# Pacing the background sums of an f32 network: the steps of three weight sums leave the leads and the widening stages

## The chip, the cores and the metric

One core of one Trainium2 chip runs the whole program. The metric is the device time of one launch in microseconds (us); the figure before is the median of three runs. The chip's engines are named as in the profile: PE (TensorE matmul), PEld (its weight load), DVE (VectorE), ACT (ScalarE), POOL (GpSimd), SP (SyncE, here only a DMA queue).

## The reference

Three transformer-like layers on 512 positions of width 1024, all in f32:

```
h = x + concat(conv_group(rmsnorm(x) @ w_in), pool_group(...)) @ w_out        # the "mixer"
h = h + swiglu(rmsnorm(h), w_gate, w_up, w_down)        # d_ff = 2816
x = rmsnorm(h)
x = layer_norm(ALPHA * x + fox_attention(x))        # first attention, 16 heads
x = layer_norm(ALPHA * x + conv_ffn(x))        # 2816 * 2 wide, 3-tap causal convolution, silu(g) * v
k1, k2, v = shared_kv(x)
x = layer_norm(ALPHA * x + diff_attention(x, k1, k2, v))        # second attention, 8 heads
x = layer_norm(ALPHA * x + conv_ffn(x))
```

So there are three feed-forward blocks. Each has a widening product (1024 to 2 x 2816) and a narrowing one (2816 to 1024).

## The kernel before

**Arithmetic.** Every f32 operand is split into a high part in fp32r (ACT, L183) and a low remainder (DVE or POOL, L185), and each product is three matmuls (L436 to L438). A weight *piece* of 128 x 1024 is converted by `_convert` into `wh` and `wl`; `piece` keeps two pieces converted ahead, and `wp` holds four. Weights arrive through `raw` buffers on the SP queue.

**Two-by-two products.** The widening and narrowing products use a seven-product scheme (seven block products in place of eight), which needs sums of blocks. On the widening side, `wide` first runs a *lead* of four chunks with plain products (`f_phase(LEAD, evac)`, tile `fa`), during which POOL builds nine sums of the activations (`sums`, tile `hT`). Then 18 chunks follow (`fast_chunk`, tiles `c` and `p`). Each of the 18 needs weight sums: one add by a DMA on POOL's queue (L274, `raw<-raw`, 512 KB) and two POOL additions (L176, `raw<-raw`).

On the narrowing side (`down`, tile `dn`) the weight sums are 32 *background steps* per feed-forward block, made by `mixed(n)`: the weights are in four quarters, and sixteen steps `copy` a quarter's part in DRAM (704 KB, ACT's queue, L145), eight steps `add` another quarter to a copied part (704 KB, an accumulating DMA on POOL's queue, L152, `mixed<-in_narrow`), and eight add one sum to another (`mixed<-mixed`). Before each `add` POOL copies one column of the newest converted piece (`paced<-wh`, L150), so that the step waits for that conversion.

**What paces the steps.** `mix` runs at the end of every `_convert`: inside `with self.mixing(pace, n)` each conversion adds `pace` to a debt, and each whole unit of debt pops one step, `n` at most (32 if not given). Outside such a block `pace` is 0 and no step is issued. All 32 steps of a block must be out before its narrowing weights are loaded (`halves`, an assert).

Before, the steps of the first sum (`mixed(0)`) are issued in the mixer (input product, output product) and then in the first block's widening stage. Those of `mixed(1)` start in the first narrowing stage (16), go on in the first attention's output product (8) and end in the next lead (8). Those of `mixed(2)` start in the second narrowing stage (16) and go on in the second attention's value product and output product (8 each).

**The mixer.** For each of four channel groups, `conv` forms a 31-tap causal convolution: a first share of the taps goes to PE as products with diagonal matrices (ACT writes them, L644 and L645, `diagonals`), a second to ACT and POOL (ACT scales, L666, `pr<-u`; POOL adds, L176, `part<-part,pr`: 10, 10, 10 and 8 of them and one more per group for PE's share), the rest to DVE (L671, `cacc`). `conv_norm` then needs all four groups (`cv`, L682), and PE's output product follows.

Instructions are put on each engine's queue by a list scheduler from the program order and priorities; an engine takes its queue in that order.

Of the kernel before, what the change touches and what calls it, by code (L numbers as in the profile page):

```python
# [25 lines left out]
KD = D // P  # L26
# [12 lines left out]
LEAD = 4  # L39
# [60 lines left out]
class Net:  # L100
# [73 lines left out]
    def pool(self, *args, **kw):  # L174

        self.pooled = self.nc.gpsimd.tensor_tensor(*args, **kw)  # L176
        return self.pooled
# [400 lines left out]
    def block1_mix(self, g):  # L578
        nc, tc, a = self.nc, self.tc, self.a
        with ExitStack() as es:  # L580
# [153 lines left out]

            with self.mixing(1):
                self.f_phase(6, evac, lead=1)
# [35 lines left out]

            with self.mixing(1):
                self.t_phase(KD, lambda k, half: ysel(k), out, order=MIX_ORDER, tail=8, pin=True)

    def wide(self, hT, evac):

        with ExitStack() as fs:
            pool, self.fz = (fs.enter_context(self.tc.tile_pool(name=n, bufs=1)) for n in ("sums", "fz"))
            with self.mixing(1):  # L780
                self.f_phase(LEAD, evac)

# [170 lines left out]
    def block1_ffn(self):  # L953
        nc, tc, a = self.nc, self.tc, self.a
        with ExitStack() as es:
            pool = lambda name, bufs=1: es.enter_context(tc.tile_pool(name=name, bufs=bufs))
            hT = pool("hT").tile([P, NF, S], F32, name="hT")
# [8 lines left out]

            with self.mixing(.5):
                self.wide(hT, evac)
            self.mixed(1)
# [5 lines left out]

            with self.mixing(.5, 16):
                self.down(es, hT, lambda x, ps, op: nc.vector.tensor_tensor(x, x, ps, op=op), done)
# [12 lines left out]
    def conv_ffn(self, layer, last):  # L990
        nc, tc, a = self.nc, self.tc, self.a
        with ExitStack() as es:
            pool = lambda name, bufs=1: es.enter_context(tc.tile_pool(name=name, bufs=bufs))
            hT = pool("hT").tile([P, NF, S], F32, name="hT")
# [16 lines left out]

            with self.mixing(.5):
                self.wide(hT, evac)
            if not last:
                self.mixed(2)
            g, b = self.row(R_FG + layer), self.row(R_FB + layer)
            done = partial(self.ln_last, g=g, b=b) if last else partial(self.ln_xt, g=g, b=b, n=1)
            with self.mixing(.5, 16):
                self.down(es, hT, lambda x, ps, op: nc.vector.scalar_tensor_tensor(x, x, ALPHA, ps, op0=ALU.mult, op1=op), done, last)
# [81 lines left out]
    def fox(self):  # L1101
        nc, tc, a = self.nc, self.tc, self.a
        with ExitStack() as es:
# [31 lines left out]

            self.t_phase(KD, lhs_v, v_out, tail=2, head=4)

# [87 lines left out]
            steps = self.fast_projections([q_done, k_done], g)  # L1225
            go = lambda n: [next(steps, None) for _ in range(n)]
# [25 lines left out]
    def diff(self):  # L1252
        nc, tc, a = self.nc, self.tc, self.a
        with ExitStack() as es:
# [122 lines left out]
            steps = chain(self.projections([q_done, k_done] * 8), begin())  # L1377
            go = lambda n: [next(steps, None) for _ in range(n)]
            go(40)
# [163 lines left out]
```

## Time and profile before

| | |
|---|---|
| median of 3 runs | 1836.85 us (1834.62 to 1841.59) |
| the profiled execution | 1831.9 us, of which the span is 1830.1 us |
| granted clock, mean | 0.974 |
| PE, DVE, ACT, POOL busy | 94%, 79%, 55%, 46% of the span |
| mixer | 16 to 185 us |
| first widening: lead, gap, 18 chunks | 184.8, 230.7, 240.8 to 449.3 us |
| first narrowing | 449 to 556 us |
| first attention, with value and output products | 556 to 828 us |
| second widening | 828.5 to 1081 us |
| second narrowing | 1081 to 1200 us |
| second attention, with value and output products | 1200 to 1464 us |
| third widening | 1464.5 to 1702.8 us |
| third narrowing | 1703 to 1817 us |

A stage's boundaries are read from the first and last matmul on its tile. The rows from the trace in the section below are of this one profiled execution. In a table by stretch the columns after the stretch are its length and, for each engine, busy us and number of instructions; the last three are the granted PE clock (1.00 is full), the mean busy share of the 16 DMA engines, and the GB/s that they moved.

### The profile page before, as it was taken

What the parts mean: (1) busy time and instruction counts of PE and PEld (TensorE: products, weight loads), DVE (VectorE), ACT (ScalarE), POOL (GpSimd) and SP (SyncE); (2) the same over time, 40 slices, a digit from 0 to 9 for tenths busy, and PEclk for the clock granted to TensorE, in tenths of its full rate; (3) what the DMA queues carried; (4) which work ended last, traced back from release to release, by engine and by line L of the source; (5) the groups of instructions that cost most, each with busy time, mean ns of one, the idle gap of its engine ahead of it and who ended that gap; (6) DMA issues with size and microseconds to landing.
All of it is one profiled execution on the core that took longest, in us unless ns stands there. A gap on an engine that the chain in (4) does not pass through costs nothing. (4 is left out here: it accounts for less than half of the span.)

```text
span 1830.1 us, 28063 instructions
## 1 busy us (share of the span) xinstructions
PE 1715.1 (94%) x10432; PEld 1500.8 (82%) x10432; DVE 1453.0 (79%) x2177; ACT 1011.7 (55%) x1733; POOL 837.1 (46%) x578
## 2 busy tenths in 40 slices
PE   7988968999999999998799999999999989999987
PEld 6767968999887788788799987777777789999865
DVE  5985544678987688878698899973888579989999
ACT  6753333455654577745365665464667455666652
POOL 2661843433506365317455555324231265655671
PEclk9998978999999999999899999999999999999999
DMA  6433788667984554666767679677333555676643
GB/s 225 149 115 138 197 183 200 191 176 224 327 269 158 136 160 131 178 158 163 175 166 194 172 241 313 236 194 203 104 96 95 137 151 137 187 191 190 204 150 112
DMA packets 106073, 326.06 MB, mean 178 GB/s; under 512 B 9888, under 2 KB 10016, under 8 KB 93904
## 3 DMA queue, kind: packets, MB, share of 16 engines
q1 hardware_dynamic: 73088, 215.53, 34.8%
q0 software_dynamic: 25648, 73.54, 21.5%
q10 hardware_dynamic: 7200, 35.20, 5.4%
q8 instruction: 82, 1.34, 0.3%
q14 instruction: 55, 0.45, 0.1%
HBM read 274.91 MB, written 73.43 MB: 190 GB/s over the span
## 5 line engine op out<-in xcount | busy, mean ns | idle before, releaser
L185 DVE TENSOR_TENSOR wl<-raw,wh 128x1024 fp32r<-128x1024 f32 (+1 forms) x415 | 561.4, 1369 | 176.7 <-ACT wh L183 173.3
L183 ACT ACTIVATE wh<-raw 128x1024 fp32r<-128x1024 f32 x457 | 449.5, 997 | 425.6 <-PE c L437 69.2
L436 PE MATMUL c<-xh,wh 128*128 128x256 f32 x992 | 288.5, 291 | 31.9 <-ACT wh L183 16.9
L176 POOL TENSOR_TENSOR raw<-raw 128x512 f32<-128x512 f32 x124 | 184.5, 1488 | 265.5 <-DMA raw<-raw 233.2
L438 PE MATMUL c<-xh,wl 128*128 128x256 f32 x992 | 285.7, 288 | 2.0 <-DVE wl L185 2.0
L437 PE MATMUL c<-xl,wh 128*128 128x256 f32 x992 | 285.0, 287 | 0.0
L436 PEld LDWEIGHTS c<-xh,wh 128*128 128x128 f32 x992 | 194.7, 196 | 35.9 <-ACT wh L183 17.7
L438 PEld LDWEIGHTS c<-xh,wl 128*128 128x128 f32 x992 | 194.8, 196 | 2.7 <-DVE wl L185 2.7
L437 PEld LDWEIGHTS c<-xl,wh 128*128 128x128 f32 x992 | 194.9, 196 | 0.1
L437 PE MATMUL dn<-wl,hh 128*128 128x512 f32 x462 | 183.1, 396 | 8.4 <-DVE wl L185 8.2
L438 PE MATMUL dn<-wh,hl 128*128 128x512 f32 x462 | 181.8, 394 | 4.3 <-DVE hl L185 4.3
L436 PE MATMUL dn<-wh,hh 128*128 128x512 f32 x462 | 181.1, 393 | 0.0
L176 POOL TENSOR_TENSOR hT<-hT 128x256 f32<-128x256 f32 (+2 forms) x66 | 147.2, 2273 | 60.1 <-DVE hT L909 54.1
L176 POOL TENSOR_TENSOR wl<-raw,wh 128x1024 fp32r<-128x1024 f32 (+1 forms) x42 | 94.3, 2250 | 117.0 <-ACT wh L183 117.0
L436 PE MATMUL fa<-xh,wh 128*128 128x256 f32 (+1 forms) x400 | 135.7, 339 | 11.5 <-DVE hT L1003 9.8
L437 PE MATMUL fa<-xl,wh 128*128 128x256 f32 (+1 forms) x400 | 134.4, 336 | 1.1 <-DVE xl L185 1.1
L438 PE MATMUL fa<-xh,wl 128*128 128x256 f32 (+1 forms) x400 | 134.2, 335 | 0.5 <-DVE rs_t L326 0.5
L176 POOL TENSOR_TENSOR rs_r<-rs_t,mhalf 128x1 f32<-128x1 f32 (+1 forms) x40 | 29.8, 747 | 226.9 <-DVE rs_t L326 223.5
L437 PEld LDWEIGHTS dn<-wl,hh 128*128 128x128 f32 x462 | 87.4, 189 | 32.8 <-DVE wl L185 15.2
L274 POOL DMA_DIRECT2D raw<-raw x62 | 76.5, 1234 | 75.5 <-DMA raw<-in_w_qk_dram 29.0
L438 PEld LDWEIGHTS dn<-wh,hl 128*128 128x128 f32 x462 | 87.6, 190 | 22.9 <-DVE hl L185 5.2
L176 POOL TENSOR_TENSOR hT<-hT,tv 128x512 f32<-128x512 f32 x44 | 82.7, 1879 | 44.7 <-DVE tv L1003 30.3
(302 smaller groups left out, 4567.2 us busy)
## 6 DMA issues: line engine op xcount, KB each, us to landing
raw<-in_w_conv_dram SPq DMA_DIRECT2D x36, 1024.0 KB, 5.0
mixed<-in_narrow_dram ACTq DMA_DIRECT2D x48, 704.0 KB, 5.7
raw<-raw POOLq DMA_DIRECT2D x62, 512.0 KB, 5.1
raw<-mixed SPq DMA_DIRECT2D x51, 512.0 KB, 5.6
raw<-in_narrow_dram SPq DMA_DIRECT2D x48, 512.0 KB, 4.9
raw<-in_w_ffn_dram SPq DMA_DIRECT2D x18, 1024.0 KB, 4.9
mixed<-in_narrow_dram POOLq DMA_DIRECT2D x24, 704.0 KB, 10.8
mixed<-mixed POOLq DMA_DIRECT2D x24, 704.0 KB, 10.3
```

Of the source, the lines that this page charges most:

```text
L176: self.pooled = self.nc.gpsimd.tensor_tensor(*args, **kw)
L183: self.copied = self.nc.scalar.activation(hi, src, AF.Copy)
L185: return self.copied, sub(lo, src, hi.bitcast(F32), op=ALU.subtract)
L274: self.nc.gpsimd.dma_start(out=raw[:, 0:4:2, :], in_=raw[:, 1:4:2, :], accum_op=ALU.add)
L436: mm(ps, lh, rh, start=first, stop=False)
L437: mm(ps, lh, rl, start=False, stop=False)
L438: mm(ps, ll, rh, start=False, stop=last)
```

## The change

The steps are the same; where they are issued changes. In the mixer the pace rises from 1 to 1.8 (input product) and 1.9 (output product), so that all 32 steps of `mixed(0)` are out before its end. The three leads and the widening stages lose their `mixing`. The narrowing stages go from pace .5 and at most 16 steps to .6 and 19. The first attention's value product gets 5 steps, and the projections in the second attention's loop run at .25.

```diff
@@ block1_mix
-            with self.mixing(1):
+            with self.mixing(1.8):
                 self.f_phase(6, evac, lead=1)
@@ block1_mix
-            with self.mixing(1):
+            with self.mixing(1.9):
                 self.t_phase(KD, lambda k, half: ysel(k), out, order=MIX_ORDER, tail=8, pin=True)
@@ wide
-            with self.mixing(1):
-                self.f_phase(LEAD, evac)
+            self.f_phase(LEAD, evac)
@@ block1_ffn and conv_ffn
-            with self.mixing(.5):
-                self.wide(hT, evac)
+            self.wide(hT, evac)
@@ block1_ffn and conv_ffn
-            with self.mixing(.5, 16):
+            with self.mixing(.6, 19):
                 self.down(...)
@@ fox
-            self.t_phase(KD, lhs_v, v_out, tail=2, head=4)
+            with self.mixing(1, 5):
+                self.t_phase(KD, lhs_v, v_out, tail=2, head=4)
@@ diff
-            go = lambda n: [next(steps, None) for _ in range(n)]
+
+            def go(n):
+                with self.mixing(.25):
+                    for _ in range(n):
+                        next(steps, None)
+
```

Two queues show where the order of the work moves. The first is POOL's at the first lead, where `hT<-hT` are the last sums of the activations, `paced` and `mixed` the background adds, and `raw<-raw` with DMA the first chunks' weight add. Before:

```order
L176 TENSOR_TENSOR hT<-hT 128x1024 x5
L150 COPY paced<-wh 128x1
L152 DMA mixed_242<-in_narrow_dram 128x1408
L150 COPY paced<-wh 128x1
L152 DMA mixed_242<-in_narrow_dram 128x1408
L150 COPY paced<-wh 128x1
L152 DMA mixed_242<-in_narrow_dram 128x1408
L150 COPY paced<-wh 128x1
L152 DMA mixed_242<-in_narrow_dram 128x1408
L274 DMA raw<-raw 128x2x512
L176 TENSOR_TENSOR raw<-raw 128x512
L274 DMA raw<-raw 128x2x512
```

And now:

```order
L176 TENSOR_TENSOR hT<-hT 128x1024 x5
L274 DMA raw<-raw 128x2x512
L176 TENSOR_TENSOR raw<-raw 128x512 x2
L274 DMA raw<-raw 128x2x512
L176 TENSOR_TENSOR raw<-raw 128x512 x2
L274 DMA raw<-raw 128x2x512
```

The four adds between the sums and the first weight add are gone, and so are the eight further ones that stood between the next chunks' adds.

The second is ACT's queue in the mixer, at the second channel group (`u_115`), whose ten scaled taps are `pr<-u_115`; `uh<-u_116` and the `dh`, `dl` rows (eight of each) belong to the third group. Before:

```order
L183 ACTIVATE uh<-u_115 128x544
L183 ACTIVATE wh<-raw 128x1024
L663 ACTIVATE part<-u_115,vec 128x512
L666 ACTIVATE pr<-u_115,vec 128x512 x5
L183 ACTIVATE wh<-raw 128x1024
L650 ACTIVATE ta<-fa,vec 128x512
L666 ACTIVATE pr<-u_115,vec 128x512 x2
L183 ACTIVATE uh<-u_116 128x544
L666 ACTIVATE pr<-u_115,vec 128x512 x3
L145 DMA mixed_242<-in_narrow_dram 128x1408
L644 ACTIVATE dh<-ident,twh 128x128
```

And now:

```order
L183 ACTIVATE uh<-u_115 128x544
L145 DMA mixed_242<-in_narrow_dram 128x1408
L183 ACTIVATE wh<-raw 128x1024
L145 DMA mixed_242<-in_narrow_dram 128x1408
L650 ACTIVATE ta<-fa,vec 128x512
L145 DMA mixed_242<-in_narrow_dram 128x1408
L183 ACTIVATE uh<-u_116 128x544
L183 ACTIVATE wh<-raw 128x1024
L663 ACTIVATE part<-u_115,vec 128x512
L644 ACTIVATE dh<-ident,twh 128x128
```

After the last row come the other fifteen diagonals and then the ten `pr<-u_115`. So the second group's taps now stand behind the third group's `uh` and its sixteen diagonals.

The third is POOL's queue in the mixer. Before, one unbroken row of 42 `part` adds stands there:

```order
L176 TENSOR_TENSOR rs_r<-rs_t,mhalf 128x1 x4
L319 DMA row<-in_rows_dram 128x1024
L176 TENSOR_TENSOR part<-part,pr 128x512 x42
L176 TENSOR_TENSOR rs_r<-rs_t,mhalf 128x1 x7
L150 COPY paced<-wh 128x1
```

And now, from the first 21 of them on:

```order
L176 TENSOR_TENSOR part<-part,pr 128x512 x21
L150 COPY paced<-wh 128x1
L152 DMA mixed_242<-in_narrow_dram 128x1408
L176 TENSOR_TENSOR part<-part,pr 128x512 x2
L150 COPY paced<-wh 128x1
L152 DMA mixed_242<-in_narrow_dram 128x1408
L176 TENSOR_TENSOR part<-part,pr 128x512 x9
L150 COPY paced<-wh 128x1
L152 DMA mixed_242<-in_narrow_dram 128x1408
L176 TENSOR_TENSOR part<-part,pr 128x512 x6
```

Three more pairs of `paced` and DMA follow before the last `part` add, so six pairs stand in the chain of the 42.

## Rows read from the trace of the kernel before

**Rows 1.** The page, part 1: busy us of each engine, share, instructions.

```profile
PE 1715.1 (94%) x10432; PEld 1500.8 (82%) x10432; DVE 1453.0 (79%) x2177; ACT 1011.7 (55%) x1733; POOL 837.1 (46%) x578
```

**Rows 2.** By stretch: first, second, third widening (lead, gap, 18 chunks; third without gap).

```profile
184.80:230.70 45.90, 45.90 (x299) 41.82 (x297) 25.23 (x19) 12.51 (x17) 34.94 (x23) 1.00 0.76 193
230.70:240.80 10.10, 0.03 (x1) 0.00 (x0) 0.02 (x1) 1.06 (x1) 1.10 (x1) 0.66 0.86 156
240.80:449.30 208.50, 196.27 (x1513) 193.32 (x1514) 136.23 (x191) 92.48 (x135) 81.31 (x71) 0.93 0.74 192
828.50:882.30 53.80, 48.17 (x299) 43.10 (x297) 36.35 (x28) 22.23 (x38) 34.78 (x26) 0.97 0.77 192
882.30:886.50 4.20, 0.09 (x2) 0.07 (x1) 1.91 (x2) 1.15 (x2) 3.12 (x2) 0.93 0.01 2
886.50:1081.20 194.70, 186.44 (x1513) 184.78 (x1514) 174.15 (x244) 116.31 (x172) 108.81 (x76) 0.98 0.67 184
1464.50:1519.40 54.90, 49.28 (x301) 44.25 (x300) 42.66 (x37) 28.25 (x45) 34.56 (x22) 0.94 0.54 136
1519.40:1702.80 183.40, 182.14 (x1513) 181.53 (x1513) 171.05 (x239) 114.06 (x166) 103.93 (x70) 1.00 0.66 184
```

**Rows 3.** Waits of PE from 230 to 320 us: total us, times, longest.

```profile
PE c L436 <- ACT wh L183: 16.9, 3, 10.1
```

**Rows 4.** Waits of PE from 880 to 910 us.

```profile
PE c L436 <- ACT m L519: 6.5, 2, 5.6
PE c L436 <- DVE hT L1003: 4.1, 1, 4.1
```

**Rows 5.** Order of time on POOL from 218 us: start us, us, what, idle before.

```profile
218.69 1.18 POOL L150 COPY paced<-wh 128x1 f32<-128x1 f32 x1
219.81 0.85 POOL L152 DMA_DIRECT2D mixed<-in_narrow_dram  x1
...
222.77 2.17 POOL L274 DMA_DIRECT2D raw<-raw  x1
239.69 1.26 POOL L176 TENSOR_TENSOR raw<-raw 128x512 f32<-128x512 f32 x1 [14.76 <-DMA raw<-raw]
```

**Rows 6.** The instructions of L274, the chunks' weight adds: issue to landing.

```profile
DMA to landing us min/median/max: 5.0/5.1/16.9
```

**Rows 7.** Order of time on ACT in the mixer.

```profile
70.55 3.16 ACT L666 ACTIVATE pr<-u,vec 128x512 f32<-128x512 f32 x5
...
79.94 0.66 ACT L183 ACTIVATE uh<-u 128x544 fp32r<-128x544 f32 x1 [2.61 <-DVE u L652]
...
82.35 0.39 ACT L644 ACTIVATE dh<-ident,twh 128x128 fp32r<-128x128 f32 x1
...
87.04 1.04 ACT L183 ACTIVATE wh<-raw 128x1024 fp32r<-128x1024 f32 x1
```

**Rows 8.** Groups on POOL from 40 to 139 us: count, busy us, mean ns, idle before.

```profile
L176 POOL TENSOR_TENSOR part<-part,pr 128x512 f32<-128x512 f32 x42 | 65.8, 1567 | 46.6 <-ACT pr L666 35.0 <-ACT pr L680 7.6 <-DVE cacc L671 1.6
```

**Rows 9.** Order of time on POOL in the mixer: second group's adds, and the last.

```profile
71.34 16.06 POOL L176 TENSOR_TENSOR part<-part,pr 128x512 f32<-128x512 f32 x10 [5.63 <-ACT pr L666]
...
136.40 1.75 POOL L176 TENSOR_TENSOR part<-part,pr 128x512 f32<-128x512 f32 x1 [3.95 <-ACT pr L680]
```

**Rows 10.** The instructions of L152, the chained background adds: issue, ns min/median/max.

```profile
L152 POOL DMA_DIRECT2D mixed<-mixed x24: 797/849/2002, 243.2 to 1474.7; - x24
```

**Rows 11.** Waits on POOL over the whole span: total us, times, longest.

```profile
POOL paced L150 <- ACT wh L183: 57.1, 14, 9.5
```

**Rows 12.** By stretch: first and second narrowing, first and second attention's output product.

```profile
449.00:556.00 107.00, 107.00 (x483) 88.81 (x482) 98.21 (x123) 64.66 (x88) 31.27 (x22) 1.00 0.85 291
1081.00:1200.00 119.00, 110.72 (x479) 88.40 (x478) 112.12 (x142) 68.86 (x97) 53.13 (x29) 0.99 0.76 260
796.00:828.50 32.50, 32.50 (x159) 27.18 (x158) 20.66 (x33) 13.56 (x26) 9.41 (x12) 1.00 0.55 135
1428.00:1464.50 36.50, 34.52 (x164) 28.36 (x165) 22.20 (x34) 15.76 (x28) 11.88 (x16) 1.00 0.69 171
```

More of the change, by code (lines that the diff above doesn't have):

```diff
@@ L1010, in evac @@
                 self.pool(g, g, v, op=ALU.mult)
-            with self.mixing(.5):
-                self.wide(hT, evac)
+            self.wide(hT, evac)
             if not last:
@@ L1017, in conv_ffn @@
             done = partial(self.ln_last, g=g, b=b) if last else partial(self.ln_xt, g=g, b=b, n=1)
-            with self.mixing(.5, 16):
+            with self.mixing(.6, 19):
                 self.down(es, hT, lambda x, ps, op: nc.vector.scalar_tensor_tensor(x, x, ALPHA, ps, op0=ALU.mult, op1=op), done, last)
```

## The prediction

> **What bounds the kernel now.** I read the page's first part, then cut the span by stage, then asked each stage that differs from its twin what PE waited for.
>
> PE is busy 94% of the span [rows 1], so time can only come out of PE's gaps and out of matmuls that run slowly. The table by stretch shows where both are. The three widening stages run the same 18 chunks (1,513 matmul records each), but their chunks take 208.5, 194.7 and 183.4 us [rows 2]. Into the first stage fall 16 background adds from just before its lead on (four at 181 to 187 us, four after the sums, eight among the chunks), into the second eight, into the third none, except the last landings of the product ahead. The first also has a gap of 10.1 us between lead and chunks and the second one of 4.2 us; the third has none. In the first, PE ran its chunks at a mean granted clock of 0.93, in the third at 1.00. So the third stage is the measured model of a widening stage without background steps.
>
> Who ends PE's waits fits that. In the first stage it is a converted weight piece (16.9 us in three waits, one of 10.1) [rows 3]. That piece waits for the first chunk's weight add, which POOL issued at 222.8 us behind four background adds, and whose landing POOL then awaited for 14.8 us [rows 5]; such an add usually lands 5.1 us after its issue, at most 16.9 [rows 6]. In the second stage PE waits 9.7 us for work on ACT and DVE that comes late in the same stretch [rows 4].
>
> **The first widening loses its 16 adds.** The weight add stands right behind the sums now. The first `paced` copy began at 218.69 us, where the sums ended; the add issues there, lands some 5.1 us later, at 224, POOL's two additions (about 1.3 us each, [rows 5]) end near 227, and the conversions need about 2.5 us more: just before the lead's end at 230.7. Then the chunks should run as in the third stage: 208.5 - 183.4 = 25.1 us, and the gap of 10.1 us: **35 us**. Bounds: if the sums still hold the first piece up (this lead is 9 us shorter than the third) the gap stays and the gain is 25; at best the chunks lose the third stage's own 1.3 us of idle PE as well, 36.5.
>
> **The second widening loses its eight.** 194.7 - 183.4 = 11.3 and the gap 4.2: **15.5 us**, of which I take 15, because its lead is 1.1 us shorter than the third's already. Bounds 11 (the gap stays) to 15.5.
>
> **The mixer pays.** It takes the 16 adds and gets its 16 copies earlier. All 16 copies were issued in the mixer already and only move up among ACT's instructions there; I cost that at nothing. The adds go on POOL into the chain of 42 `part` adds, which ends at 138.15 us [rows 9] and behind which PE waits for the normalisation. Two things lengthen it.
>
> First, ACT's order. The second group's ten scaled taps began at 70.55 and POOL's adds on them at 71.34 [rows 7, 9]. Now they stand behind the third group's `uh` (at 79.94 before; some 2.5 us sooner now, as one of DVE's weight remainders no longer stands between the second and the third group's inputs), one conversion, the `part` start and sixteen diagonals (82.35 to 87.04, 4.7 us): 77.4 + 0.7 + 1.0 + 0.8 + 4.7 + 0.7 = 85.3 us, 14 us later.
>
> Second, the pairs. From there POOL has 31 adds of 1.567 us [rows 8], 48.6 us, and six pairs of `paced` and DMA; a pair costs from about 1.1 us back to back to 2.0 behind an addition (1.18 + 0.85, [rows 5]), so 10 us at 1.7. That ends at 144 us if POOL never waits, 6 us later than now. It will wait: the first pair needs a conversion that now follows the next sixteen diagonals on ACT, and I give that 5 us and later feeding 2. Last add at 151: **13 us later**. POOL idled 46.6 us before these 42 adds [rows 8], so the cover may be larger than I think: the lower bound is 0. The upper is 21, if the 15 us of idle time that stood between the later adds all stays as well.
>
> PE cannot fill the delay, since the output product's second part needs all four groups. The pairs behind the last add come before the row statistics, which then waited for DVE anyway; they cost nothing as long as that wait covers them, and 1.7 us each if not.
>
> Here a rule speaks against the change. The issue of an add takes POOL 0.85 us at the median and 2.0 us at the longest [rows 10], also in the second widening, where DVE was busy 174 of 195 us [rows 2]. The Trainium skill, page "SBUF — State Buffer", section "SBUF: two separate sides", says that a DMA issued on POOL's queue cannot get its descriptors written while DVE runs an operation in a mode with two ports, with 620 ns growing to 3100 ns. By that rule 16 issues beside the mixer's busy DVE would cost, as an estimate from that page, 16 x 2.5 = 40 us in place of 13. The trace bears it out at most to 2.0 us.
>
> **The small ones.** The first value product gets five adds, three of them ahead of the first weight add of the projections: 3 x 1.7 = 5 us later there, plus a landing of up to 12 us more. The projections start only after the forget gate's product, which covers nearly all of it: 1 us, bounds 0 to 6. The two narrowing stages issue their 16 copies over some 27 conversions instead of 32, and three adds each: the first runs at a DMA share of 0.85 with PE never idle, the second has 8.3 us of idle PE [rows 12]. I take 1 us for both together, bounds 0 and 16 (both with as much more idle as the second has now). The first attention's output product gets the chained adds that the second's had: 32.5 us for 159 matmul records against 36.5 for 164, PE idle 0 against 2.0 [rows 12]. So 2 us go to the first, and 2 come back from the second, which loses seven of its eight. The four steps in the second attention's loop lie beside a full PE and cost nothing; if that cover is gone, 4 x 2 us.
>
> **Sum** against the profiled execution: 1831.9 - 35 - 15 + 13 + 1 + 1 + 2 - 2 = 1797. That execution lies 5 us under the median of the runs (1836.85), so the same difference of -35 gives **1802** for a median. Its own range, with the mixer at 4 to 20 and the first gain at 30 to 36: 1793 to 1813.
>
> **Rivals.**
>
> *The mixer hides it all* (chance 0.15). POOL's 46.6 us of idle time speak for it [rows 8], ACT's new order against. The mixer's term falls to 2: -46, 1791.
>
> *The narrowing stages become DMA-bound* (0.10). The first one's share of 0.85 [rows 12] speaks for it; that the second, at 0.76, loses more shows that DMA is not what stops it. Twice 8.3 us: -35 + 16 = -19, 1818.
>
> *The first lead keeps its stall* (0.07). The sums end 12 us before the lead does, and the first pieces fit with little to spare. The gap of 10 us stays and half of the chunks' gain: -35 + 10 + 12 = -13, 1824.
>
> *POOL's issues are held up by DVE* (0.05). The longest issue was 2.0 us against 0.85 at the median [rows 10]: 16 x 1.2 = 19 us more on the chain: -16, 1821. The rule of the Trainium skill above is of this mechanism; the price here is that of the rows.
>
> *Slower: the paced copies wait in the chain* (0.05). Each of the six pairs ahead of the last `part` add waits for a conversion, and that conversion for PE to free a buffer, and PE for the chain. The longest such wait was 9.5 us [rows 11]; six of them are 57 us, with the 13 above 70, against gains of 50: +20, 1857. It decides once the last add ends later than about 188 us. Against it: the mean of the 14 waits is 4.1 us, and the conversions they name are mostly done before POOL gets there.
>
> **How the numbers follow.** The forecast has 0.55; the rivals 0.42; 0.03 is left for what I do not see. The range must reach from the hidden mixer (with a little more, 1785) past 1818 and 1821 to 1824; it leaves out the slower case, the unseen and the outer parts of the others, some 0.15. A measurement of this kernel tells a difference from none at about 0.5%, 9 us: faster means below 1828. Forecast, hidden mixer, narrowing and most of the two next cases lie there: 0.89; within 0.5%: 0.06; slower: 0.05.
>
> **What would show it.** In the first widening: no gap between lead and chunks, chunks at 183 to 186 us and clock 1.00, the first weight add issued where the sums end and landed in 5 us. In the second: chunks at 183 to 185. In the mixer: POOL's second group of adds starts near 85 us, the last `part` add ends near 151, and the lead starts some 13 us later than 184.8. The narrowing stages keep 107 and 119 us. I am wrong if the mixer ends more than 21 us later, or if the chunks of the first widening still take over 195 us.

## The result, and the profile after

The changed kernel takes **1804.74 us** (median of 4 runs, 1801.63 to 1808.99) against 1835.99 for the kernel before (4 runs, 1834.62 to 1841.59): ratio **0.9825, interval 0.9806 to 0.9843**. The forecast was 1802.0, within 1785 to 1824.

The execution that was profiled took 1808.99 us (span 1807.2), the longest of the four, and its twin of before 1831.9, under all four of its runs. So the two traces differ by 22.9 us where the medians differ by 31.25. The stages below are of the traces.

The page, part 1, of the changed kernel (compare [rows 1]):

```profile
PE 1704.6 (94%) x10432; PEld 1490.4 (82%) x10432; DVE 1459.6 (81%) x2177; ACT 1017.0 (56%) x1733; POOL 842.2 (47%) x578
```

Then the table by stretch, in the columns of [rows 2]. The lines are: first lead, first chunks, first narrowing; second lead, chunks and narrowing; third lead and chunks.

```profile
190.30:236.50 46.20, 45.96 (x300) 42.02 (x298) 30.68 (x23) 16.86 (x23) 32.34 (x16) 1.00 0.60 160
236.50:417.90 181.40, 181.40 (x1513) 181.40 (x1512) 133.20 (x186) 90.19 (x131) 66.66 (x52) 1.00 0.67 187
417.90:529.10 111.20, 108.33 (x480) 89.37 (x479) 95.69 (x123) 65.00 (x87) 37.92 (x27) 0.98 0.88 299
811.60:858.60 47.00, 46.25 (x300) 42.08 (x298) 34.87 (x34) 27.75 (x45) 35.70 (x17) 1.00 0.49 136
858.60:1046.50 187.90, 182.97 (x1513) 181.73 (x1512) 174.61 (x240) 113.96 (x167) 106.03 (x70) 1.00 0.64 181
1046.50:1177.60 131.10, 114.03 (x480) 91.28 (x479) 114.02 (x143) 69.33 (x98) 58.71 (x35) 0.93 0.77 253
1446.30:1493.30 47.00, 46.28 (x300) 42.12 (x299) 34.86 (x34) 27.72 (x45) 35.46 (x16) 1.00 0.38 110
1493.30:1679.70 186.40, 182.62 (x1514) 181.65 (x1512) 175.41 (x241) 114.57 (x167) 101.11 (x70) 1.00 0.66 182
```

The first chunks now keep PE busy for all of their 181.4 us at full clock, where before they took 208.5 us at 0.93 after a gap of 10.1 us. On POOL's timeline at the first lead this is the cause, against [rows 5]:

```profile
216.23 6.73 POOL L176 TENSOR_TENSOR hT<-hT 128x1024 f32<-128x1024 f32 x2
222.90 1.21 POOL L274 DMA_DIRECT2D raw<-raw  x1
228.58 3.55 POOL L176 TENSOR_TENSOR raw<-raw 128x512 f32<-128x512 f32 x2 [4.46 <-DMA raw<-raw]
232.07 1.20 POOL L274 DMA_DIRECT2D raw<-raw  x1
```

The weight add stands right behind the sums, lands 4.46 us after its issue ended (14.8 us before), and the chunks begin as the lead ends, at 236.5.

All stages together, each from its first matmul to that of the next, in us. The columns besides before and the change are kernels of the next section, each named for what it holds; a profiled execution each.

| stage | before | change | 1st sum only | 2nd only | 3rd only | change, narrow .5 | 1st+2nd | 1st + out2 |
|---|---|---|---|---|---|---|---|---|
| mixer, to the lead | 184.8 | 190.3 | 191.3 | 185.2 | 184.8 | 190.7 | 192.4 | 192.5 |
| first lead (with gap) | 56.0 | 46.2 | 46.2 | 56.1 | 56.0 | 46.2 | 46.2 | 46.2 |
| first chunks | 208.3 | 181.4 | 181.4 | 209.2 | 211.3 | 181.4 | 181.4 | 181.4 |
| first narrowing | 106.5 | 111.2 | 107.4 | 108.5 | 106.9 | 107.0 | 111.1 | 106.5 |
| first value product | 49.8 | 50.5 | 51.3 | 50.5 | 49.7 | 51.9 | 50.5 | 51.4 |
| first attention | 191.2 | 200.1 | 192.9 | 198.2 | 191.9 | 200.6 | 197.0 | 192.6 |
| its output product | 31.9 | 31.9 | 31.9 | 31.9 | 31.9 | 31.9 | 31.9 | 31.9 |
| second lead (with gap) | 58.0 | 47.0 | 57.9 | 47.0 | 58.2 | 47.0 | 47.0 | 47.0 |
| second chunks | 194.5 | 188.0 | 194.2 | 187.2 | 194.4 | 187.9 | 187.7 | 186.9 |
| second narrowing | 119.5 | 131.1 | 118.3 | 119.8 | 128.8 | 119.9 | 119.4 | 119.4 |
| second value product | 46.2 | 46.5 | 46.3 | 46.2 | 46.5 | 46.2 | 46.3 | 46.3 |
| second attention's loop | 181.8 | 188.2 | 181.8 | 181.8 | 195.3 | 193.5 | 181.8 | 181.8 |
| its output product | 36.1 | 34.0 | 36.4 | 36.6 | 34.0 | 36.2 | 37.9 | 36.3 |
| third lead | 54.7 | 47.0 | 54.4 | 54.6 | 46.9 | 47.0 | 54.6 | 54.7 |
| third chunks | 183.5 | 186.4 | 182.3 | 185.5 | 186.2 | 186.8 | 183.4 | 183.4 |
| third narrowing | 114.4 | 114.4 | 114.4 | 114.4 | 116.1 | 116.1 | 116.1 | 114.4 |

Each column is one execution. How far a stage varies by itself is seen in five kernels whose queues are the same on every engine up to the second narrowing stage: the change, and those of the next section with the first two sums, with the pace alone, with the copies, and with the loop's filling free of steps. Between them the leads, the chunks and the first narrowing stage come back within 0.5 us. But the mixer takes 190.2 to 192.4, the value product 50.5 to 53.1, and the first attention 192.5 to 200.1 us, with the same instructions in the same order. The second narrowing stage varies by 2 to 3 us between kernels whose queues are the same there (131.1 and 128.5; 119.4 and 121.2), and the loop without steps takes 181.8 in each column. So a difference of 4 us is to be believed in most stages; in the first attention a single execution shows nothing under 8 us.

From before to the change: the three widening stages give back 36.7, 17.5 and 4.8 us, the second output product 2.1; the mixer takes 5.5, the two narrowing stages 16.3, the value products 1.0, the first attention 8.9 and the second's loop 6.4. That is 61.1 - 38.1 = 23.0, the whole difference of the traces.

### The profile page after: what moved, and what is told of

Same layout as the page of the kernel before. It is cut to its first block, busy times and chain, and to the rows that moved or that the text cites. A ratio compares the mean times of both kernels' runs of the same rounds, so it can differ in the third digit from the quotient of the medians.

```text
span 1807.2 us, 28083 instructions
## 1 busy us (share of the span) xinstructions
PE 1704.6 (94%) x10432; PEld 1490.4 (82%) x10432; DVE 1459.6 (81%) x2177; ACT 1017.0 (56%) x1733; POOL 842.2 (47%) x578
## 5 line engine op out<-in xcount | busy, mean ns | idle before, releaser
L436 PE MATMUL c<-xh,wh 128*128 128x256 f32 x992 | 284.0, 286 | 13.4 <-ACT m L519 10.6
L176 POOL TENSOR_TENSOR raw<-raw 128x512 f32<-128x512 f32 x124 | 178.7, 1441 | 246.8 <-DMA raw<-raw 214.0
L438 PE MATMUL c<-xh,wl 128*128 128x256 f32 x992 | 281.3, 284 | 0.0
L437 PE MATMUL c<-xl,wh 128*128 128x256 f32 x992 | 281.3, 284 | 0.0
L436 PEld LDWEIGHTS c<-xh,wh 128*128 128x128 f32 x992 | 190.7, 192 | 16.5 <-ACT m L519 13.0
L437 PEld LDWEIGHTS c<-xl,wh 128*128 128x128 f32 x992 | 190.9, 192 | 0.1
L438 PEld LDWEIGHTS c<-xh,wl 128*128 128x128 f32 x992 | 190.9, 192 | 0.0
L176 POOL TENSOR_TENSOR hT<-hT 128x256 f32<-128x256 f32 (+2 forms) x66 | 155.3, 2378 | 68.0 <-DVE hT L908 67.9
L437 PEld LDWEIGHTS dn<-wl,hh 128*128 128x128 f32 x462 | 88.7, 192 | 36.4 <-DVE wl L185 18.4
L438 PEld LDWEIGHTS dn<-wh,hl 128*128 128x128 f32 x462 | 88.7, 192 | 31.9 <-DVE hl L185 13.9
L274 POOL DMA_DIRECT2D raw<-raw x62 | 74.8, 1206 | 69.8 <-DVE wl L185 23.7
L176 POOL TENSOR_TENSOR hT<-hT,tv 128x512 f32<-128x512 f32 x44 | 87.3, 1984 | 37.0 <-DVE tv L1001 22.6
```

What stands on the lines that cost most here:

```text
L274: self.nc.gpsimd.dma_start(out=raw[:, 0:4:2, :], in_=raw[:, 1:4:2, :], accum_op=ALU.add)
L436: mm(ps, lh, rh, start=first, stop=False)
L437: mm(ps, lh, rl, start=False, stop=False)
L438: mm(ps, ll, rh, start=False, stop=last)
```

## The experiments

Theory: the leads and widening stages gain what was forecast, and a good part of it is paid back where the steps now are, more than forecast outside the mixer. Rival: the three sums matter little apart from the first, and the longer narrowing and attention stages are chance.

**One sum at a time.** Each kernel is that of before with one sum's edits; the steps that are left for a lead or a widening stage are then none, so its `mixing` there does nothing.

```diff
# e1_sum1: mixer            mixing(1) -> mixing(1.8) and mixing(1.9)
# e2_sum2: block1_ffn down  mixing(.5, 16) -> mixing(.6, 19)
+            with self.mixing(1, 5):        # first value product
                 self.t_phase(KD, lhs_v, v_out, tail=2, head=4)
# e3_sum3: conv_ffn down    mixing(.5, 16) -> mixing(.6, 19); diff: go() at mixing(.25)
```

First sum. 

> Before, with the mixer's two paces (1.8 and 1.9) alone; the second and third sums stay as they were. Theory A (nearly the whole net gain is the first sum's): first widening 264 -> 228 us, mixer +5.5 as in the trace of the change, so -31 us, about 1805. Rival B (the prediction's mixer term, +13): -22 us, about 1814. If the gain needed the second sum's move as well: above 1820.

Measured: 1806.11 us against 1838.32, ratio 0.9841 (0.9819 to 0.9863). That is 32 us between the medians and 29 by the ratio, near theory A: the first sum alone is nearly the net gain.

Second sum. 

> Before, with the second sum's move alone (first narrowing .6/19, five steps in the value product; its eight chained adds then all fit in the output product, none in the second lead). Theory A (the narrowing stage and the first attention really cost what the changed kernel's trace shows, +4.7 +0.7 +8.9, against -17.6 in the second widening): -3 us, about 1833, no change that can be measured. Rival B (those costs are scatter of one execution or come from elsewhere, the prediction's -15 +1 +0.5 +2): -11 us, about 1825.

Measured: 1829.22, ratio 0.9954 (0.9937 to 0.9971), 9 us. That is between, nearer to rival B. By stage the second lead and chunks gain 18.3 us, theory A's 17.6; the narrowing pays 2.0, and the first attention 7.0, which is no more than it varies by itself.

Third sum. 

> Before, with the third sum's move alone (second narrowing .6/19, the second attention's loop at .25). Theory A (trace of the change: second narrowing +11.7, loop +6.5, output product -2.1, third widening -4.8): +11 us, about 1847. Rival B (prediction: +0.5 and -2, the loop free): -1 us, about 1835.

Measured: 1851.85, ratio **1.0077** (1.0059 to 1.0095), 13.5 us **slower**. Rival B falls. The narrowing stage pays 9.3 us and the loop 13.5, twice what the change's trace shows there. The third lead gains 7.8.

**Taking the third sum's move out.** The first and second moves of the change, the third sum as before.

> The first and second sums' moves as in the change, the third sum as before. Theory A (the third sum's move is a loss of its own, 1851.85 against 1838.32 in the runs so far): the ratios of the first two moves alone multiply, 0.9841 x 0.9954 = 0.9796, some 1798 to 1800, under the change. Rival B (the three moves do not add up, the change's 1805 is what two of them give as well): 1804 to 1808.

Measured: 1798.09 against 1836.24, ratio 0.9797 (0.9780 to 0.9815), as theory A has it. So the change would have been 5 us better without its third part (0.9825 against 0.9797). The intervals just overlap, but the stages agree: from the second narrowing stage to the end the table has 747.6 us for the change and 739.5 here. The third part costs less here than by itself (13.5), as the loop loses 6.4 in the change and 13.5 alone.

**The narrowing stages: faster copies, or the three adds?** First the change with the narrowing stages as before:

```diff
-            with self.mixing(.6, 19):      # block1_ffn and conv_ffn
+            with self.mixing(.5, 16):
-            with self.mixing(1, 5):        # first value product
+            with self.mixing(1, 8):
```

> The change with both narrowing stages back at pace .5 and 16 steps, and eight steps in the first value product, so that the second sum is still out before its lead. Theory A (the faster pace and the three adds are what made the narrowing stages longer): both return to 107 and 119 us, 12 to 16 us under the change, about 1790. Rival B (their length is scatter, or comes from the schedule for other reasons): within 4 us of the change, about 1805.

Measured: 1803.25, ratio 0.9814 (0.9794 to 0.9834). Both narrowing stages return to 107.0 and 119.9 us, as theory A has it, but the time does not follow: in this kernel the value product with eight steps and the loop cost more (1.4 + 5.3 us, and 2.2 in the second output product, which gets the three adds that left the narrowing stage). Why the loop's same four adds cost more here is shown below.

Then the faster pace without the adds, on the kernel of 1798.09:

```diff
-            with self.mixing(.5, 16):      # conv_ffn
+            with self.mixing(.6, 16):
```

> As the run before (first two moves, third sum as before), with the second narrowing's sixteen copies at .6 in place of .5, but none of the three adds. Theory A (the faster pace alone puts DVE's and POOL's work in another order there, and that costs): second narrowing 129 to 131 us in place of 119, the whole some 10 us slower than the run before. Rival B (the three adds on POOL cost it): second narrowing stays at 119 to 121 us.

Measured: 1801.36, ratio 0.9829 (0.9810 to 0.9847); second narrowing 124.6 us, between the two: 3 to 5 us of the 11.6 come from the pace alone (the same stage at the old pace takes 119.4 and, in a second kernel with these queues, 121.2). PE's waits in that stage are here mostly one wait, and the changed kernel has the same one. The second line is of this kernel, the third of the changed one:

```profile
PE dn L438 <- DVE hl L185: 10.2, 1, 10.2
PE dn L437 <- DVE wl L185: 2.5, 3, 1.9
PE dn L437 <- DVE wl L185: 6.0, 4, 3.5
```

The timelines of DVE and POOL in the changed kernel show what it is:

```profile
1111.97 1.27 DVE L848 TENSOR_TENSOR X<-X,dn 128x512 f32<-128x512 f32 x2
1113.17 1.27 DVE L1016 SCALAR_TENSOR_TENSOR X<-X,dn 128x512 f32<-128x512 f32 x2
1114.36 6.91 DVE L185 TENSOR_TENSOR hl<-hT,hh 128x512 fp32r<-128x512 f32 x1
```

```profile
1113.13 0.63 POOL L319 DMA_DIRECT2D row<-in_rows_dram  x1
1113.77 6.94 POOL L422 TENSOR_TENSOR X<-X,row 128x1024 f32<-128x1024 f32 x3
```

The activation's low part `hl`, for which PE waits, begins 0.6 us after POOL's three additions of the bias row have begun. It takes 6.91 us, until these are done, where the next `hl` takes 0.68. In the kernel of 1798.09 DVE's order is another there (a `wl` stands directly ahead of this `hl`, not four additions `X<-X,dn`): `hl`, `wl` and `hl` get in between POOL's three additions at 2.85, 3.40 and 2.85 us, these take 9.43, and PE waits 2.9 and 1.9 us. So other copies among the conversions give another order on DVE, and with it another meeting of the two engines. Behind the wait PE runs slower for a while; the table by stretch of the changed kernel has, for the wait itself and the 9.7 us after it:

```profile
1111.10:1121.30 10.20, 0.03 (x1) 0.00 (x0) 10.20 (x7) 1.30 (x2) 9.88 (x6) 0.73 0.72 260
1121.30:1131.00 9.70, 9.68 (x33) 7.88 (x34) 7.53 (x9) 3.17 (x4) 0.31 (x1) 0.75 0.58 184
```

The rest comes with the three adds. Between the kernel with the pace alone and the changed one nothing else differs on any queue there; PE, ACT and DVE have the same order to the end. With the adds PE has one wait more, of 3.5 us for a `wl` on DVE (6.0 in place of 2.5 in the lines above). The three kernels traced with the three adds all have it (3.5, 3.5 and 3.6 us, some 114 us into the stage), and no other has. A second execution of the changed kernel's queues took 128.5 us in this stage, so some 2.6 of the 131.1 are not the adds': its waits of `dn` are the same, and PE is busy 110.4 us in place of 114.0, at a granted clock of 0.96 in place of 0.93. In the kernel with the third sum alone the 9 us lie in four waits of 1.7 to 4.2 us. How an add on POOL makes DVE's `wl` late was not taken apart.

**The loop: the copy's wait, or the transfer?** Four paced copies in the loop that no add follows, on the kernel of 1798.09:

```diff
     def mix(self):
+        if self.probe:                     # set in the second attention's loop
+            self.probe += 1
+            if self.probe % 4 == 1:
+                m = self.sm.tile([P, 1], F32, name="paced", tag="paced")
+                self.nc.gpsimd.tensor_copy(m, self.ready[-1][0][:, 0:1].bitcast(F32))
```

> As the first run of this group, with four paced copies in the second attention's loop, at every fourth conversion, that no add follows (all eight adds stay in the output product). Theory A (the loop's loss comes from the 704 KB of each add's transfer, which delays the loop's small transfers zs, qh and kh): the loop from the last value product to the end of the output product stays at 182 us. Rival B (the copies' waits on POOL, ahead of the weight remainders, cost it): 188 to 195 us.

Measured: 1798.55, ratio 0.9798 (0.9785 to 0.9811). The 182 us is the stretch from the first projection to the *start* of the output product (the expectation says "end" by mistake), and it stays: 181.9. The copies waited 18.7 us for conversions and cost nothing, so the add itself costs: its transfer, or the 0.85 us that POOL takes to issue it, which no run separates. Next, the change without an add in the loop's first forty calls:

```diff
-            go(40)
+            for _ in range(40):
+                next(steps, None)
```

> The change, with no step in the first forty calls of the second attention's projections (where its first heads are filled in), and .25 from there on, so that no add is issued before the loop proper. Theory A (what the loop's adds cost is one collision: the first add's transfer with the first heads' zs, qh and kh, on which PE waits while nothing else is there to do): from the first projection to the start of the output product 182 to 184 us in place of 188, the whole some 5 us under the change's 1805, about 1800. Rival B (each add costs its share wherever it lies): 186 us or more, at most 2 us under the change.

Measured: 1809.33, ratio 0.9831 (0.9805 to 0.9856): no gain over the change. The loop takes 188.3 us, as in the change, so theory A falls. Only three of its adds are now issued in the loop (43, 85 and 129 us after the first projection; the fourth has moved into the output product), so that is 2.1 us for each, against 1.6 for each of the change's four. The table by stretch for the loop, first with the copies alone, then with the adds:

```profile
1209.20:1391.10 181.90, 178.88 (x905) 133.47 (x903) 136.04 (x303) 115.54 (x304) 51.42 (x30) 1.00 0.39 108
```

```profile
1221.50:1409.80 188.30, 180.87 (x903) 133.51 (x902) 140.36 (x303) 114.67 (x304) 56.43 (x32) 1.00 0.44 115
```

In this last kernel, DVE's wait and the landing times of the same transfer's line:

```profile
DVE zs L1287 <- DMA zs<-z: 27.2, 6, 19.3
```

```profile
DMA to landing us min/median/max: 1.9/2.0/7.2
```

These two are of `zs<-z`, the rotary product's exchange of rows by 64 transfers of 64 KB: with adds DVE waits for it six times in place of three (23.9 us in the kernel without), and its longest landing is 7.2 us in place of 5.6. PE is idle 7.4 us in place of 3.0. In the change PE waits for such a transfer itself, at 82.8 and 125.9 us after the first projection, as the adds of 74.8 and 118.5 land; with the copies alone it never does:

```profile
PE sc L1093 <- DMA kh<-kl: 1.0, 2, 0.6
```

So the transfers are late beside an add, but these two waits are 1.0 of the 6.4 us; the rest was not followed from transfer to wait.

The collision that theory A meant exists, but in other kernels: where the first add falls 14.6 us after the first projection (third sum alone, and the change with narrowing at .5), the first head's `kh` is late. PE's wait for it in the kernel with the third sum alone, and a stretch that begins 3 us behind it in the table by stretch:

```profile
PE sc L1096 <- DMA kh<-kl: 2.0, 1, 2.0
```

```profile
1292.60:1302.00 9.40, 9.17 (x23) 5.85 (x23) 9.28 (x23) 5.50 (x15) 0.55 (x1) 0.50 0.58 173
```

After the wait PE ran these 9.4 us at 0.50, the lower of its two clocks (1.2 GHz). In the change the first add falls at 9.1 us and this wait is missed: 188.2 us against 195.3 and 193.5, with four adds in each.

**The mixer: the same steps behind the chain.** On the kernel of 1798.09:

```diff
-            with self.mixing(1.8):   # f_phase        mixing(1)
-            with self.mixing(1.9):   # t_phase        mixing(2.9)
```

> As the first run of this group, with the mixer's paces at 1 and 2.9 in place of 1.8 and 1.9: the same 32 steps, but ACT's and POOL's order ahead of the output product as before, and two pairs instead of six ahead of the last part add. Theory A (the mixer's 5.5 us come from the pairs and ACT's order in the chain of part adds): the lead starts at 185 to 187 us, the whole 3 to 5 us faster than the first run. Rival B (it comes from elsewhere, or the adds that now crowd behind the chain delay the normalisation): no faster, or slower by up to 5 us.

Measured: 1798.37, ratio 0.9798 (0.9778 to 0.9817). Both are right in part: the lead starts at 185.4 us, so what the mixer lost came from the pairs and ACT's order ahead of the chain's end; but the lead then takes 52.8 us in place of 46.2, with one wait of PE, about which DVE's and POOL's timelines tell the rest:

```profile
PE pt L337 <- DVE y L357: 5.1, 1, 5.1
```

```profile
197.96 1.28 DVE L357 SCALAR_TENSOR_TENSOR y<-X,rs_r,row 128x1024 f32<-128x1024 f32 x1 [8.44 <-POOL rs_r L176]
```

```profile
196.52 0.81 POOL L152 DMA_DIRECT2D mixed<-mixed  x1 [3.61 <-issue]
197.07 0.86 POOL L176 TENSOR_TENSOR rs_r<-rs_t,mhalf 128x1 f32<-128x1 f32 x1
```

`y` is the normalised row that the next block turns, and its scale `rs_r` stands on POOL behind adds that follow each other closely, three of which POOL issues late (2.2, 2.4 and 3.6 us of idle time). The profile names no cause for the last two, but the landings do. These are steps that add one sum to another, and they read a sum that an earlier step has written. Three of those earlier steps, issued at 163.4 to 164.7 us, take long to land:

```profile
DMA to landing us min/median/max: 20.1/23.1/26.7
```

The second and third of them land at 187.14 and 191.42 us, the one after them at 196.04; the three late steps start at 187.62, 191.91 and 196.52, each 0.48 or 0.49 us behind. So a step that must wait for its input holds up all that stands behind it on POOL. What the chain gains the lead gives back.

**The first widening: gap and chunks apart.** Before, with the first lead's `mixing` set to 0; fourteen adds then lie among the chunks, two ahead of the lead and none in it.

> Before, with no steps in the first lead alone: the sixteen steps that are left after the mixer are then issued among the first chunks (twelve or more adds there in place of eight, none between the sums and the first weight add). Theory A (an add among the chunks costs in proportion, 25 us for eight): the gap of 10 us goes and the chunks grow by 10 or more, no change in all, 1830 to 1845. Rival B (the chunks' loss in before is the aftermath of the late first weight add): gap gone and chunks near 195 or less, 1815 to 1820.

Measured: 1833.12, ratio 0.9964 (0.9949 to 0.9978). Lead and chunks of this kernel:

```profile
187.60:233.90 46.30, 45.92 (x299) 42.02 (x297) 29.61 (x23) 16.38 (x22) 31.55 (x14) 1.00 0.49 138
233.90:445.80 211.90, 196.17 (x1514) 192.47 (x1513) 131.84 (x187) 88.13 (x132) 91.40 (x80) 0.94 0.82 208
```

The gap is gone and the chunks take 211.9 us. Rival B falls; theory A has the time, but not the proportion. Fourteen adds cost 30.5 us over the 181.4 of the change, 2.2 us each on average, yet only 3.6 more than the eight of before. In both kernels PE is busy 196.2 us, at a mean granted clock of 0.94 and 0.93, for the work that takes 181.4 at 1.00: some 15 us, the same for eight adds as for fourteen. Only the rest, PE's idle time, differs: 15.7 us here, 12.2 before. What eight adds would cost without the late first weight add was not measured.

How an add costs is seen in the chunks' weight adds, which follow it on POOL's queue. Their landings, before and in the change:

```profile
DMA to landing us min/median/max: 5.0/5.0/16.9
DMA to landing us min/median/max: 5.0/5.0/5.6
```

In the change all 18 take 5.0 to 5.6 us. Before, five take 6.8 to 16.9, four of these within 4 us behind background adds; in the kernel with fourteen, seven behind such adds take 6.3 to 15.9.

**Better places.** If the narrowing stage and the value product cost, and the output product does not:

```diff
# before, with the mixer at 1.8 and 1.9, and in fox:
-            with self.mixing(1):           # output product
+            with self.mixing(2):
```

> The first sum's move as in the change; of the second, the narrowing stage as before (.5/16), nothing in the value product, and all sixteen adds in the first attention's output product at pace 2; the third as before. Theory A (the adds in the narrowing stage and the value product cost 4 and 7 us, the output product, where POOL is busy 9 of 32 us, takes sixteen as it takes eight): narrowing 107, first attention 186 to 188 us, about 11 us under the 1798 of the two moves, 1787. Rival B (sixteen adds in 32 us hold the normalisation or the second lead up): product or lead longer by 8 us or more, no faster than 1796.

Measured: **1790.69** against 1838.91, ratio **0.9737** (0.9709 to 0.9765): faster than both kernels, 0.9 points under the change, between the two theories and nearer to theory A. Of its stages the narrowing is as theory A has it, the first attention is not (192.6 us, not 186 to 188). Narrowing, output product and second lead of this kernel:

```profile
420.20:526.70 106.50, 106.50 (x479) 88.33 (x479) 97.12 (x123) 64.37 (x87) 31.77 (x21) 1.00 0.85 292
770.70:802.60 31.90, 31.90 (x156) 26.62 (x154) 20.70 (x33) 13.61 (x26) 11.78 (x18) 1.00 0.97 226
802.60:849.50 46.90, 46.18 (x298) 42.05 (x297) 34.59 (x33) 27.47 (x45) 36.63 (x19) 1.00 0.55 151
```

Not all sixteen adds fall in the output product: eight are issued in the last 38 us of the attention (from 732.3 us on), seven in the product and one as the lead begins. In the product the DMA engines are busy 0.97 and PE is never idle. Beside the adds only three transfers are issued in it, all of weights (256 and 1024 KB): nothing small. Last, the same with the third sum's last adds out of the third lead:

```diff
-            with self.mixing(1):           # diff, output product
+            with self.mixing(1.5):
```

> The run before (first sum in the mixer, second sum's adds all in the first output product), with the second attention's output product at pace 1.5 in place of 1: the third sum's last add, which stands between the third lead's activation sums on POOL, and the one ahead of it move up before the normalisation's last rows; on the other engines nothing moves. Theory A (an add among a lead's sums delays the first weight add, and PE with it): third lead 47 in place of 54.9 us, chunks 183.5 to 186.6, about 5 us under the run before's 1790, near 1785. Rival B (the third lead's length has another cause): 54 to 55 us, no change.

Measured: 1789.69 against 1835.87, ratio 0.9738 (0.9711 to 0.9766), no change. The lead does fall to 47.0 us and the chunks rise to 186.9, as theory A has it, but the output product rises from 36.3 to 42.2 us. PE's waits around the lead, before this edit and after it:

```profile
PE fa L436 <- DVE hT L1003: 4.9, 1, 4.9
```

```profile
PE c L436 <- ACT m L519: 2.8, 1, 2.8
```

and in the output product a gap of 5.75 us ahead of the normalised rows, in place of 2.14. The cause is the mixer's: three adds there, which read the sums that the first three write, start 0.48 or 0.49 us after those have landed (1.9, 4.9 and 4.4 us of idle time on POOL), and the rows' scale `rs_r` stands behind them. Behind the gap the mean granted clock is 0.87 to the end of the product.

## Why the prediction was right, and where it was not

The time and its sign were right, and the largest step nearly exactly. But several smaller terms were wrong in both directions and cancelled, so that 1802 came within 3 us of 1804.74 is in part luck.

**First widening, -35.** Measured -36.7, its upper bound 36.5 and a little more: no gap, chunks 181.4 us with PE never idle, the weight add where the sums end. The split was too simple: I took the chunks' 25.1 us as what eight adds cost, but fourteen cost hardly more, and some 15 us of it is PE running slower in either kernel.

**Second widening, -15.** Measured -17.5 (lead 11, chunks 6.5). The gap of 4.2 goes and the lead's own stall with it; the chunks take 188.0 us, not 183 to 185, and PE waits 2.7 us for ACT at their start.

**Third widening, not forecast.** -4.8: its lead loses 7.7, since the third sum's adds are nearly all out before it, and its chunks take 2.9 more. I had called this stage free of background steps "except the last landings of the product ahead"; the last add itself stood among its sums, issued at 1474.7 us [rows 10]. So the stage that served as the model had a loss of its own, in its lead.

**The mixer, +13.** Measured +5.5, within the bounds of 0 and 21 (5.4 to 8.2 in the nine kernels with these paces). The order was forecast well and so were the waits; the work was taken too long. POOL's timeline shows the second group, the waits and the chain's end:

```profile
83.43 14.01 POOL L176 TENSOR_TENSOR part<-part,pr 128x512 f32<-128x512 f32 x10 [16.05 <-ACT pr L666]
101.67 0.32 POOL L150 COPY paced<-wh 128x1 f32<-128x1 f32 x1 [4.23 <-ACT wh L183]
...
109.40 14.76 POOL L176 TENSOR_TENSOR part<-part,pr 128x512 f32<-128x512 f32 x9 [2.66 <-ACT pr L666]
...
143.01 1.52 POOL L176 TENSOR_TENSOR part<-part,pr 128x512 f32<-128x512 f32 x1
```

The second group starts at 83.43 (85.3 in the forecast), six pairs stand ahead of the last add, the first pair waits 4.23 us for its conversion (5 in the forecast), and later one group of adds waits 2.66 (2 in the forecast). But the last add ends at 144.5, not 151. Of the 6.5 us the start has 1.9; the six pairs take 7.4 us in place of 10, and the 31 adds 46.9 with the gaps between them, in place of 48.6. That 144.5 is nearly the forecast's "144 us if POOL never waits" is chance, as POOL did wait. The rival in which DVE holds POOL's issues up falls too: the fifteen issues up to 190 us took 0.85 us at the median and 1.59 at the longest, and the 40 us of the rule that spoke against the change did not come. So does the slower case: the longest wait of a paced copy ahead of the chain's end was 4.2 us, not 9.5, and there was one, not six.

**The value product, +1.** Measured in the trace +0.7 in the product and 8.9 in the first attention behind it, over my bound of 6. But this execution is the longest of five with the same queues. Product and attention together take 246 to 251 us in those five, 248 in the mean, and 241 to 245 in the six kernels with no step in the product, 243 in the mean. So the adds cost some 5 us in place of 1, within the bound. The step that was too small is that the forget gate's product "covers nearly all of it". The landing that I had set at up to 12 us more came: POOL's first weight add of the projections landed 18.0 us after its issue, 5.1 in the kernel with the first sum alone. In the eight kernels with steps in the value product it takes 15.9 to 18.1 us, in the six without 5.1. POOL's sums and weight remainders shift by some 15 us, and the trace shows what they then meet. PE waits 2.8 us for `va` on DVE as the chunks begin. Five of the eight kernels with steps have this wait at 2.1 to 2.9 us, those without do not have it. Later, on POOL and on DVE:

```profile
575.71 3.58 POOL L176 TENSOR_TENSOR raw<-raw 128x512 f32<-128x512 f32 x2 [13.82 <-DMA raw<-raw]
...
629.09 5.11 POOL L176 TENSOR_TENSOR wl<-raw,wh 128x1024 fp32r<-128x1024 f32 x2
```

```profile
628.40 6.09 DVE L1188 TENSOR_SCALAR p<-p,re 128x512 f32<-128x512 f32 x1
```

The softmax's scaling took 6.09 us beside two of POOL's remainders (1.97 in the kernel with the first sum alone), and PE waited 3.5 us for what follows it. The other kernels with five steps there do not have this wait, and take 192.5 to 198.6 us: it belongs to this execution, not to the change.

**Both narrowing stages, +1.** Measured +16.3, just past the bound of 16 (4.7 in the first, 11.6 in the second, of which 2.6 are the execution's). The rival that had 16 for them gave the DMA engines as the reason; they are not it, as the second stage has a share of 0.77 at 131.1 us, 0.76 before [rows 12], and PE's waits there name DVE. The failed step is that the faster copies and the three adds were taken to cost nothing there: the copies move the order of DVE and ACT, which a scheduler sets, and PE waits 10.2 us in one place; the adds bring one more wait of 3.5 us.

**The loop, 0.** Measured +6.4, and 11.7 and 13.5 in two variants. The failed step is "lie beside a full PE and cost nothing": PE, idle 3.0 us there without adds, is idle 6.1 with them. The price given for the case that the cover is gone, 4 x 2 us, was near. The small transfers, 2.0 us at the median, take up to 7.9 us in the change; that this is the whole cause is not shown.

**The output products, +2 and -2.** 0 and -2.1.

So -35 in the sum was -23.0 in the traces (and -31 in the medians, whose profiled members lie at opposite ends): 7.5 us too much set down for the mixer and 7.3 too little for the gain of the second and third stages (and 3.8 in smaller terms) stand against 15.3, 8.6 and 6.4 too little for narrowing, first attention and loop (and 0.3). The change's trace also holds the longest first attention and the longer second narrowing of those with the same queues, so it shows more loss than the medians do.

## What to carry to other kernels

A busy DMA share does not tell whether background work costs. In this program the end of an attention and its output product took sixteen adds at a DMA share of 0.97 with PE never idle in the product, while three or four adds in a loop at a share of some 0.4, with its many 64 KB transfers, cost 6 us. Test each move by itself: of the three here one gave 29 us, one 9, and one lost 13.5, which their sum hid. Before you read a difference of one stage, look for runs with the same queues there: the first attention varied by 7.6 us between such runs. Where a scheduler orders the queues, look at what else it moves: an order on DVE that nobody edited cost 3 to 5 us. And a background step that reads an earlier one's result holds its whole queue until that has landed.

## What the runs showed of the hardware

A 0.68 us addition on DVE took 6.91 us beside three additions of 6.94 us on POOL, and 6.90 beside 6.93 in the kernel with the pace alone. The Trainium skill, page "SBUF — State Buffer", section "SBUF: two separate sides", says that an operation of DVE with two inputs in SBUF and one of POOL that reads SBUF share a pair of ports, which one of them holds for a whole instruction while the other waits. The trace agrees here, and shows that a row of POOL's instructions can keep DVE out for all of them. In the kernel of 1798.09, three instructions of DVE got in between POOL's three. The 6.09 us in the first attention fit less well: that operation of DVE has one input beside a column of scalars, had begun 0.69 us ahead of the first of POOL's two, and still ended 0.3 us after the second.

An add of 704 KB from DRAM to DRAM costs by its surroundings: nothing that the trace shows in the first output product, 2.2 us among the first chunks (the mean of fourteen), 1.6 to 2.1 in the loop, and 5 to 7 more in the two kernels whose first add meets the loop's first transfers.

A weight add of 512 KB on the same queue landed 5.0 to 5.6 us after its issue in first chunks without adds of 704 KB, and up to 15.9 us behind such adds; ahead of the first attention it took 5.1 us without them and up to 18.1 behind them.
